# A Hymba layer on one core: units of the feed-forwards in a new input order, FFN1's down groups of 3, 4 and 4, and the final norm's scaling taken from PSUM

## The chip, the core and the metric

The kernel runs on one core of one Trainium2 chip. The metric is the device time of one execution in microseconds; the kernel before takes 996.2 us (median of 3 runs, 993.84 to 996.5). A core has five engines that each work through their own instructions in order: TensorE (PE; its weight loads are listed as PEld), VectorE (DVE), ScalarE (ACT), GpSimd (POOL) and SyncE (SP, which here only issues DMAs). They wait for each other through semaphores. Matrix products go from SBUF into banks of PSUM.

## What is computed

One decoder layer on 528 tokens (16 learned meta tokens ahead of 512 inputs) of width 1024, everything in fp32:

```
def swiglu_ffn(h, w_gu, w_down):
    gate, up = jnp.split(h @ w_gu, 2, axis=-1)
    return (jax.nn.silu(gate) * up) @ w_down          # hidden width 2816

h = concatenate([meta, x])
h = h + 0.5 * swiglu_ffn(rms_norm(h, ffn1_norm), ffn1_w_gu, ffn1_w_down)      # FFN1
h = h + hybrid_mixer(rms_norm(h, mix_norm), w_in, conv_w, b_f, ..., w_out)    # convolution + attention
h = h + 0.5 * swiglu_ffn(rms_norm(h, ffn2_norm), ffn2_w_gu, ffn2_w_down)      # FFN2
return rms_norm(h[:, 16:], final_norm)
```

The change is in FFN1, FFN2 and the final norm. The mixer between them (convolution, attention with forget gates, output projection) is not touched.

## The kernel before

**Products.** Activations lie transposed, features on the 128 partitions, tokens in the free dimension. A product in fp32 is made of three matmuls on rounded parts: every operand is split into a high part `hi` and a rest `lo` (`w_hi`, `w_lo` for weights), and hi·hi, hi·lo and lo·hi are added in PSUM. The split of a weight tile is one cast on ScalarE (`w_hi`) and one subtraction on VectorE (`w_lo`). The weights are loaded in each run by SP's DMAs into `raw` tiles.

**Units.** Most of the two feed-forwards is computed in units by Winograd's form of Strassen's scheme: a block of 2x2 sub-blocks with 7 products instead of 8, of which each works on sums of sub-blocks. The tokens are the halves of one side (264 each in FFN1, 256 in FFN2), two neighbouring column tiles of the weights the other. A unit of gates or of ups contracts four pairs of feature tiles (`nj` = 4, 12 matmuls a product); a down unit contracts `nj` pairs of hidden tiles for two output tiles (`m`), so a group of four units covers the width. FFN1 before has a group of 3 pairs after the hidden tiles 6 to 7, a second of 3, then one of 2 and one of 3 at the end.

The weights of a unit come in four versions (`prep`): `nat` (as loaded), `s1`, `s3` and `s24`. Sums are made partly by DMA, partly by VectorE: SP loads the block (`load`), ScalarE copies one quarter of it (`base`, L474), two DMAs on GpSimd's queue add a second quarter onto `s1` and `s3` (`add`, L478), VectorE makes `s2` (L481) and `s4` (L484), and each version is split (`hi` L492, `lo` L496). Between the products ScalarE copies partial results in PSUM with the sign changed: B = -A (L535) and C = -B (L536); TensorE then adds onto these copies. The other operand, sums ("forms") of hidden tiles, is made in `pair_forms` by GpSimd (L379 to L382) and split by L368 and L369.

The first hidden tiles of each feed-forward (`classical`) are computed by ordinary products (L318) with 4 slots each, since the norm's statistics aren't ready yet; meanwhile VectorE prepares the normed input (`x_pair`, L398).

**What sets the order.** `Slots` is an order written by hand. A product of a unit is a slot, a unit has seven (b is its first; the last product of the unit before stands in slot b+1). `sl.at(t, fn, prio)` puts work of the other engines behind slot t, sorted by prio. As every engine takes its instructions in order, an instruction that waits holds up all that stands behind it on its engine. `prep` counts its steps from b: load at b-15, base b-11, add b-10, s2 b-2, s4 b-1, the split of `s24` at b (cast) and b+1 (rest). Tiles come from pools with few buffers: four for `w_hi` and `w_lo`, three for `raw`, two for `s3`.

**The end of FFN1.** After the last down units `fin` prepares the mixer's input for each finished tile of hT: a cast L275 on ScalarE, then L280 on VectorE, a square L289 on ScalarE and its addition L290 on GpSimd.

**The end of the kernel.** The last two hidden tiles of FFN2 are multiplied in four blocks of 128 tokens (L1210). `finish` then takes the row sums of squares (L1222, ScalarE), the multiplication by the norm's gain out of PSUM (L1224, VectorE), the factor r = 1/rms (L1226, L193, L296 to L298), the scaling by r (L1230 on ScalarE for the left half, L1232 on VectorE for the right half), and the output DMAs (L1233), one on ScalarE's queue and one on SP's.

## Time and profile before

| | |
|---|---|
| median of 3 runs | 996.2 us (993.84, 996.2, 996.5) |
| the profiled execution | 994.59 us, of which its span in the trace is 992.6 |
| busy share of the span | PE 96%, DVE 79%, ACT 59%, POOL 35% |
| granted TensorE clock, mean | 0.989 |

The profiled execution is 1.6 us shorter than the median; 2.0 us of it lie around the span. Times in the trace count from the start of the span. FFN1 lasts until about 386 us, the mixer until about 600, FFN2 until about 966, and the rest is the end. A row of a timeline is one or several like instructions on one engine: start, busy time, engine, line, what is written and read, their number, and in brackets how long the engine stood idle before and what ended that. "PEclk" is the granted clock as a share of full speed. TensorE's matmuls overlap, so its busy share is high even while it isn't at its best; its idle time is what has to be looked at.

### The profile page before, as it was taken

Reading aid. Unit: us, or ns where it says so; the run is one execution under the profiler, and the core shown is the slowest. Engines: PE = TensorE matmul, PEld = TensorE weight load, DVE = VectorE, ACT = ScalarE, POOL = GpSimd, SP = SyncE. Lnnn points to the kernel's source line nnn. Section 1 sums busy time; section 2 is a strip of 40 time slices with the busy share of each in tenths; the row PEclk is TensorE's granted clock in tenths of the full one; section 3 lists DMA queues with packets and bytes.
Section 4 is the critical chain, followed back from the end, with each engine's and each line's share of the span. In section 5 each row is a group of like instructions: output and inputs, shape, how many; then the busy total and the mean of one; then the engine's idle time right before and its main releaser. Section 6 shows DMA issues by size and latency. Waiting matters only on the chain.

```text
span 992.6 us, 17859 instructions
## 1 busy us (share of the span) xinstructions
PE 948.9 (96%) x7022; PEld 905.7 (91%) x7022; DVE 780.0 (79%) x1260; ACT 583.3 (59%) x1036; POOL 345.6 (35%) x319
## 2 busy tenths in 40 slices
PE   9898999999999898999999999999999999999994
PEld 8798999999999887989899978778999999999993
DVE  5688887888788887786777666778887888788764
ACT  5545655665576564775656665446555665667444
POOL 4347533543444563100000000266443553354300
PEclk9999999999999999999999999999999999999998
DMA  6237488668784571532222221247778668787712
GB/s 194 65 107 145 118 174 159 148 120 181 171 151 97 117 142 32 144 103 60 74 66 78 57 84 43 64 137 151 138 157 190 132 133 181 146 180 149 174 29 86
DMA packets 173188, 121.01 MB, mean 122 GB/s; under 512 B 5844, under 2 KB 171520, under 8 KB 173104
## 3 DMA queue, kind: packets, MB, share of 16 engines
q1 hardware_dynamic: 113376, 89.37, 29.6%
q0 software_dynamic: 59008, 28.93, 23.9%
q10 hardware_dynamic: 720, 1.57, 0.4%
q8 instruction: 55, 0.90, 0.4%
q14 instruction: 29, 0.24, 0.1%
HBM read 117.69 MB, written 2.10 MB: 121 GB/s over the span
## 4 chain that ended last, share of the span: by engine, by line
PE 73%; DVE 15%; ACT 5%; issue 4%; DMA 1%; POOL 1%; SPq 0%; ACTq 0%; DVEq 0%
PE bank L522 47%; PE bank L318 20%; DVE w_lo L496 4%; DVE arena L369 2%; PE bank L1055 2%; DMA raw<-in_ffn_w_gu_dram 1%; DVE hT L604 1%; PE bank L1210 1%; DVE w_lo L454 1%; PE bank L992 1%; PE bank L1022 1%; ACT arena L275 1%; DVE w_lo L81 1%; DVE xn L398 1%; PE acc L318 1%
## 5 line engine op out<-in xcount | busy, mean ns | idle before, releaser
L522 PE MATMUL bank<-arena,w_hi 128*128 128x256 f32 (+1 forms) x3080 | 567.7, 286 | 13.3 <-ACT bank L536 7.7
L522 PEld LDWEIGHTS bank<-arena,w_hi 128*128 128x128 f32 x3080 | 481.7, 191 | 19.7 <-ACT bank L536 11.4
L522 PE MATMUL bank<-arena,w_lo 128*128 128x264 f32 (+1 forms) x1540 | 439.1, 285 | 4.2 <-DVE w_lo L496 4.2
L522 PEld LDWEIGHTS bank<-arena,w_lo 128*128 128x128 f32 x1540 | 294.6, 191 | 5.5 <-DVE w_lo L496 5.2
L492 ACT CAST w_hi<-raw 128x1024 fp32r<-128x1024 f32 (+2 forms) x186 | 176.3, 948 | 137.1 <-DVE raw L484 109.7
L318 PE MATMUL bank<-arena,w_hi 128*128 128x264 f32 (+2 forms) x1152 | 246.6, 322 | 2.6 <-ACT w_hi L450 2.6
L496 DVE TENSOR_TENSOR w_lo<-raw,w_hi 128x1024 fp32r<-128x1024 f32 (+2 forms) x186 | 222.9, 1199 | 25.8 <-ACT w_hi L492 24.2
L318 PEld LDWEIGHTS bank<-arena,w_hi 128*128 128x128 f32 x1152 | 178.9, 190 | 18.4 <-ACT w_hi L450 3.0
L318 PE MATMUL bank<-arena,w_lo 128*128 128x264 f32 (+2 forms) x576 | 155.0, 323 | 5.3 <-DVE w_lo L454 5.3
L318 PEld LDWEIGHTS bank<-arena,w_lo 128*128 128x128 f32 x576 | 96.2, 190 | 15.8 <-DVE w_lo L454 8.2
L478 POOL DMA_DIRECT2D raw<-in_ffn_w_gu_dram x34 | 44.1, 1297 | 82.2 <-DMA raw<-in_ffn_w_gu_dram 81.2
L478 POOL DMA_DIRECT2D s<-in_ffn_w_gu_dram x34 | 50.6, 1489 | 61.0 <-ACT bank L536 60.2
L80 ACT CAST w_hi<-raw 128x1024 fp32r<-128x1024 f32 (+3 forms) x54 | 44.1, 828 | 45.9 <-PE bank L318 36.0
L81 DVE TENSOR_TENSOR w_lo<-raw,w_hi 128x1024 fp32r<-128x1024 f32 (+2 forms) x53 | 55.3, 1052 | 18.0 <-ACT w_hi L80 17.7
L478 POOL DMA_DIRECT2D s<-in_ffn_w_down_dram x28 | 41.2, 1472 | 69.1 <-ACT bank L536 63.5
L604 DVE TENSOR_TENSOR hT<-bank,hT 128x264 f32<-128x264 f32 (+1 forms) x112 | 47.5, 424 | 14.9 <-PE bank L522 14.1
L496 DVE TENSOR_TENSOR w_lo<-s,w_hi 128x512 fp32r<-128x512 f32 (+2 forms) x62 | 46.8, 755 | 0.0
L193 ACT ACTIVATE s<-s 128x256 f32<-128x256 f32 (+3 forms) x42 | 19.3, 460 | 46.1 <-DVE s L561 26.7
L474 ACT COPY s<-raw 128x512 f32<-128x512 f32 (+2 forms) x62 | 35.5, 572 | 18.5 <-DVE w_lo L496 15.6
L481 DVE TENSOR_TENSOR raw<-raw 128x512 f32<-128x512 f32 (+2 forms) x62 | 41.4, 669 | 0.8
L369 DVE TENSOR_TENSOR arena<-ts,arena 128x1056 fp32r<-128x1056 f32 (+1 forms) x29 | 35.9, 1237 | 7.5 <-ACT arena L368 7.5
L478 POOL DMA_DIRECT2D raw<-in_ffn_w_down_dram x28 | 35.4, 1264 | 15.2 <-DMA raw<-in_ffn_w_down_dram 14.5
(229 smaller groups left out, 1158.0 us busy)
## 6 DMA issues: line engine op xcount, KB each, us to landing
raw<-in_ffn_w_gu_dram SPq DMA_DIRECT2D x34, 1024.0 KB, 7.0
raw<-in_ffn_w_down_dram SPq DMA_DIRECT2D x20, 768.0 KB, 4.4
raw<-in_w_in_dram SPq DMA_DIRECT2D x24, 512.0 KB, 4.0
raw<-in_ffn_w_gu_dram POOLq DMA_DIRECT2D x34, 256.0 KB, 4.7
s<-in_ffn_w_gu_dram POOLq DMA_DIRECT2D x34, 256.0 KB, 6.3
raw<-in_ffn_w_gu_dram SPq DMA_DIRECT2D x16, 512.0 KB, 4.0
raw<-in_ffn_w_down_dram SPq DMA_DIRECT2D x4, 1024.0 KB, 5.1
raw<-in_ffn_w_down_dram POOLq DMA_DIRECT2D x20, 192.0 KB, 4.4
```

Of the source, the lines that this page charges most:

```text
L80: nc.scalar.copy(h, src)
L81: nc.vector.tensor_sub(lw, src, h.bitcast(F32))
L318: nc.tensor.matmul(ap, lhsT=wt[:, kw, :], rhs=mt[:, k, c0 - off:c1 - off], start=(first and a == 0 and b == 0), stop=(last and a == len(ks ...
L369: self.sl.at(t + 1, lambda: nc.vector.tensor_sub(lo, src(), hi.bitcast(F32)), 2)
L474: nc.scalar.copy(raw["s3"], raw["all"][:, 0::2, 0])
L478: nc.gpsimd.dma_start(out=t, in_=mat_j[:, i, :, c0 + P:c0 + 2 * P], accum_op=ALU.add)
L481: nc.vector.tensor_add(raw["all"][:, 0::2, 0], raw["all"][:, 0::2, 1], raw["all"][:, 0::2, 0])
L492: nc.scalar.copy(w[nm_][0][:, :m], src(nm_))
L496: nc.vector.tensor_sub(w[nm_][1][:, :m], src(nm_), w[nm_][0][:, :m].bitcast(F32))
L522: nc.tensor.matmul(bank, lhsT=wt[:, idx(j), :], rhs=r[:, form, part], start=(start and i == 0), stop=(i == last), skip_group_check=True)
L604: return lambda: nc.vector.tensor_add(t, ps, t)
L1055: nc.tensor.matmul(oo, lhsT=lt, rhs=rt, start=(a == 0 and n_ == 0), stop=(a == 1 and n_ == len(ops) - 1))
```

## The change

1. **Inside a unit** (`prep`): `base` and `add` come two slots later, `s2` and `s4` and the split of `s24` one slot sooner. In the first unit of each feed-forward `nat`, `s2`, `s4` and `s24` come one further slot sooner.
2. **Classical weights** (`prep_classical`): load, cast and rest three slots sooner.
3. **FFN1's opening**: the pool of FFN1 is opened earlier; the weights of hidden tile 2 are loaded in the first stage and split there (`split_raw2`); the gains are transposed and copied sooner.
4. **FFN1's groups**: down groups of 3, 4 and 4 pairs instead of 3, 3, 2 and 3, that is 12 units instead of 16. The gates of tile 14 stand ahead of the second group, its ups behind it. The forms of the last hidden pair are made by `last_pair`, its sums on VectorE, directly ahead of the last group, whose first unit takes its products in the order T2, B21, T1 instead of B21, T2, T1 (`late`).
5. **FFN2's end**: the last two weight tiles are loaded 12 and 11 slots sooner, and split 2 slots sooner.
6. **`finish`**: in the first three blocks r is applied together with the gain, in one VectorE instruction out of PSUM for each half; the output DMAs go to SP, except the left half of the last block.

```diff
-            self.sl.at(t - 8, load, 3)
-            self.sl.at(t - 2, hi, 3)
-            self.sl.at(t - 1, lambda: nc.vector.tensor_sub(w["w"][1], w["r"], w["w"][0].bitcast(F32)), 3)
+            self.sl.at(t - 11, load, 3)
+            self.sl.at(t - 5, hi, 3)
+            self.sl.at(t - 4, lambda: nc.vector.tensor_sub(w["w"][1], w["r"], w["w"][0].bitcast(F32)), 3)
...
             sl.at(b - 15, load, 3)
-            sl.at(b - 11, base, 3)
-            sl.at(b - 10, add, 3)
-            sl.at(b - 2, s2, 3)
-            sl.at(b - 1, s4, 3)
-            for nm_, t in (("nat", b - 4), ("s24", b), ("s1", b + 1), ("s3", b + 2)):
+            sl.at(b - 9, base, 3)
+            sl.at(b - 8, add, 3)
+            c = b - 1 if self.p4 is None else b
+            sl.at(c - 3, s2, 4)
+            sl.at(c - 2, s4, 3)
+            for nm_, t in (("nat", c - 4), ("s24", c - 1), ("s1", b + 1), ("s3", b + 2)):
...
+            for p in (p6, p2, p5) if late else (p2, p6, p5):
+                sl.slot(p)
...
+        def last_pair(self, j, b):
...
+            def split(f, n, s, t):
+                hi, lo = (r[:, f:f + n, i] if n > 1 else r[:, f, i] for i in range(2))
+                sl.at(t, lambda: nc.scalar.copy(hi, s()), 0)
+                sl.at(t + (f in (F_B22, F_T1)), lambda: nc.vector.tensor_sub(lo, s(), hi.bitcast(F32)), 0)
...
+            split(F_B11, 1, lambda: src(0, 0), b + 3)
+            split(F_B22, 1, lambda: src(1, 1), b + 6)
+            sl.at(b + 7, sums, 0)
+            split(F_T1, 3, lambda: v["t"][:, :3], b + 7)
+            sl.at(b + 9, lambda: nc.vector.tensor_sub(v["t"][:, 3], src(1, 0), v["t"][:, 1]), 0)
+            split(F_B21, 1, lambda: src(1, 0), b + 9)
+            split(F_T4, 1, lambda: v["t"][:, 3], b + 9)
...
+            wts2 = [split_raw2(0)]
+            row_rstd(sa)
             table(SILU_SET)
+            out_of(a3)
+            wts2.append(split_raw2(1))
...
         g_units(range(8, 14))
+        F.gates(14)
         for m in range(0, ND, 2):
-            F.down(3, 3, m)
-        g_units(range(14, NF))
+            F.down(3, 4, m)
+        t = F.ups(14)
+        F.hidden_pair(7, t, t)
+        g_units(range(16, NF - 2))
+        F.gates(NF - 2)
+        F.ups(NF - 2)
+        F.last_pair(NF // 2 - 1, len(sl.pe) - 7)
         for m in range(0, ND, 2):
-            F.down(6, 2, m)
-        for m in range(0, ND, 2):
-            for i, t in enumerate(F.down(8, 3, m)):
+            for i, t in enumerate(F.down(7, 4, m, m == 0)):
...
-                sl.at(n - 10 + 6 * i, W.load, 4)
-                sl.at(n - 4 + 3 * i, lambda: W.split(False), 4)
+                sl.at(n - 22 + 7 * i, W.load, 4)
+                sl.at(n - 6 + 3 * i, lambda: W.split(False), 4)
...
-                    nc.vector.tensor_mul(zs[b], pss[i][b], gb[:, b * 512:(b + 1) * 512])
+                    if i == 3:
+                        nc.vector.tensor_mul(zs[b], pss[i][b], gs[b])
...
-                    if b == 0:
+                    if i < 3:
+                        stt(zs[b], pss[i][b], r, gs[b], ALU.mult, ALU.mult)
+                    elif b == 0:
                         nc.scalar.mul(zs[b], zs[b], r)
...
-                    (nc.scalar, nc.sync)[b].dma_start(out=out[i * P:(i + 1) * P, b * 512:(b + 1) * 512], in_=zs[b])
+                    (nc.scalar if i == 3 and b == 0 else nc.sync).dma_start(out=out[i * P:(i + 1) * P, b * 512:(b + 1) * 512], in_=zs[b])
```

**ScalarE in FFN1's first group of three pairs.** In the kernel before, these rows stand on ScalarE in one unit (L474 is the base copy of a later unit, L536 is C = -B, L589 a copy out of PSUM, L535 the next B = -A):

```order
L492 CAST w_hi<-s_1033 128x512
L492 CAST w_hi<-raw 128x768
L474 COPY s_1277<-raw 128x384
L536 ACTIVATE bank<-bank 128x264
L589 COPY ssum<-bank 128x264
L492 CAST w_hi<-raw 128x768
L535 ACTIVATE bank<-bank 128x264
```

The changed kernel has on ScalarE in the same place (L499 is the base copy, L564 C = -B, L617 the copy out of PSUM, L563 B = -A):

```order
L517 CAST w_hi<-s_1068 128x512
L517 CAST w_hi<-raw 128x768
L564 ACTIVATE bank<-bank 128x264
L617 COPY ssum<-bank 128x264
L499 COPY s_1309<-raw 128x384
L517 CAST w_hi<-raw 128x768
L563 ACTIVATE bank<-bank 128x264
```

The base copy moved from the place ahead of C = -B to the second place behind it.

**VectorE in the last units of FFN1.** In the kernel before, VectorE has these rows in a unit of the last group (L604 are additions into hT, L280 is `fin`'s, the first L496 is the rest of `s24`, the second that of `s1`; names with their numbers):

```order
L604 TENSOR_TENSOR hT_67<-bank_517,hT_67 128x264
L280 SCALAR_TENSOR_TENSOR arena_70<-hT_67,gains_75,arena_70 128x528
L496 TENSOR_TENSOR w_lo_4240<-raw_4061,w_hi_4239 128x768
L604 TENSOR_TENSOR hT_67<-bank_515,hT_67 128x264
L496 TENSOR_TENSOR w_lo_4257<-raw_4061,w_hi_4256 128x768
L604 TENSOR_TENSOR hT_67<-bank_514,hT_67 128x264
L280 SCALAR_TENSOR_TENSOR arena_70<-hT_67,gains_75,arena_70 128x528
```

In the changed kernel VectorE has these (L632 additions into hT, L521 the rests of `s24` and `s1`, now of four pairs):

```order
L632 TENSOR_TENSOR hT_67<-bank_532,hT_67 128x264
L521 TENSOR_TENSOR w_lo_4039<-raw_3790,w_hi_4038 128x1024
L280 SCALAR_TENSOR_TENSOR arena_70<-hT_67,gains_75,arena_70 128x528
L632 TENSOR_TENSOR hT_67<-bank_530,hT_67 128x264
L521 TENSOR_TENSOR w_lo_4076<-raw_3790,w_hi_4075 128x1024
L632 TENSOR_TENSOR hT_67<-bank_529,hT_67 128x264
L280 SCALAR_TENSOR_TENSOR arena_70<-hT_67,gains_75,arena_70 128x528
```

The rest of `s24` has moved ahead of L280.

**VectorE in FFN1's opening.** Before, VectorE goes from the norm's factor (L297, L298) to the first classical weights (L454) and the first hidden tiles (L749 to L754) in this order:

```order
L297 SCALAR_TENSOR_TENSOR tt<-sm,tt 128x264
L298 SCALAR_TENSOR_TENSOR rs<-tt,y_482 128x264
L454 TENSOR_TENSOR w_lo<-raw,w_hi 128x1024
L749 SCALAR_TENSOR_TENSOR raw<-raw,rs 128x528
L753 SCALAR_TENSOR_TENSOR raw<-raw,rs 128x528
L754 TENSOR_TENSOR raw<-raw 128x528
L749 SCALAR_TENSOR_TENSOR raw<-raw,rs 128x528
L753 SCALAR_TENSOR_TENSOR raw<-raw,rs 128x528
L754 TENSOR_TENSOR raw<-raw 128x528
L454 TENSOR_TENSOR w_lo<-raw,w_hi 128x1024
L423 SCALAR_TENSOR_TENSOR s<-bank,rs 128x264 x2
```

In the changed kernel VectorE has there (L748 are the two weight tiles split in the first stage, L794 to L799 the first hidden tiles, L479 the next classical weights):

```order
L305 TENSOR_TENSOR arena<-ssum,arena 128x528
L748 TENSOR_TENSOR w_lo<-raw,w_hi 128x1024
L297 SCALAR_TENSOR_TENSOR tt<-sm,tt 128x264
L298 SCALAR_TENSOR_TENSOR rs<-tt,y_501 128x264
L297 SCALAR_TENSOR_TENSOR tt<-sm,tt 128x264
L298 SCALAR_TENSOR_TENSOR rs<-tt,y_501 128x264
L794 SCALAR_TENSOR_TENSOR raw<-raw,rs 128x528
L748 TENSOR_TENSOR w_lo<-raw,w_hi 128x1024
L798 SCALAR_TENSOR_TENSOR raw<-raw,rs 128x528
L799 TENSOR_TENSOR raw<-raw 128x528
L794 SCALAR_TENSOR_TENSOR raw<-raw,rs 128x528
L798 SCALAR_TENSOR_TENSOR raw<-raw,rs 128x528
```

The first rest of a weight tile has moved ahead of the norm's factor, the second one ahead of the first hidden tile's product.

## Rows read from the trace of the kernel before

**Rows 1.** The page: busy time by engine, and one group of instructions with its mean
```profile
PE 948.9 (96%) x7022; PEld 905.7 (91%) x7022; DVE 780.0 (79%) x1260; ACT 583.3 (59%) x1036; POOL 345.6 (35%) x319
...
L496 DVE TENSOR_TENSOR w_lo<-raw,w_hi 128x1024 fp32r<-128x1024 f32 (+2 forms) x186 | 222.9, 1199 | 25.8 <-ACT w_hi L492 24.2
```

**Rows 2.** Stretches: length, then each engine's busy us (count), clock, DMA share, GB/s
```profile
37.20:92.00 54.80, 50.73 (x393) 49.43 (x392) 45.09 (x62) 25.39 (x36) 28.13 (x25) 0.97 0.44 114
92.00:105.00 13.00, 10.53 (x74) 10.31 (x73) 11.20 (x14) 8.35 (x15) 7.71 (x9) 0.87 0.68 119
325.00:386.00 61.00, 52.26 (x399) 49.23 (x397) 52.81 (x98) 35.90 (x67) 31.02 (x30) 1.00 0.54 105
386.00:390.00 4.00, 4.00 (x18) 3.67 (x17) 4.00 (x7) 0.91 (x3) 1.73 (x1) 0.57 0.00 0
610.00:674.90 64.90, 60.63 (x260) 47.85 (x259) 54.79 (x71) 34.92 (x51) 26.89 (x24) 1.00 0.35 95
674.90:687.30 12.40, 10.33 (x73) 10.13 (x72) 11.04 (x13) 6.96 (x12) 8.10 (x7) 0.86 0.70 127
717.60:752.10 34.50, 33.64 (x275) 32.88 (x274) 30.56 (x55) 19.60 (x34) 14.97 (x12) 1.00 0.74 161
913.20:953.60 40.40, 40.40 (x338) 40.38 (x337) 32.23 (x48) 21.05 (x31) 10.65 (x7) 1.00 0.67 138
980.00:992.60 12.60, 0.00 (x0) 0.00 (x0) 4.62 (x12) 5.55 (x16) 0.00 (x0) 0.64 0.33 125
```

**Rows 3.** All waits of an engine by what ended them: us, times, longest
```profile
PE bank L522 <- ACT bank L536: 7.7, 16, 1.2
...
PE bank L522 <- ACT bank L535: 4.9, 3, 2.5
PE bank L522 <- DVE w_lo L496: 4.2, 4, 1.8
```

**Rows 4.** Timeline around 225: start, us, engine, line, operation [idle before <-releaser]; ACT, then PE
```profile
224.72 0.51 ACT L474 COPY s<-raw 128x384 f32<-128x384 f32 x1 [1.00 <-DVE w_lo L496]
...
225.57 0.52 PE L522 MATMUL bank<-arena,w_hi 128*128 128x264 f32 x2 [0.47 <-ACT bank L536]
...
226.04 0.41 PE L522 MATMUL bank<-arena,w_hi 128*128 128x264 f32 x2
```

**Rows 5.** Timeline at the first unit of FFN1: VectorE, then ScalarE
```profile
91.39 2.11 DVE L481 TENSOR_TENSOR raw<-raw 128x512 f32<-128x512 f32 x1
93.53 1.12 DVE L484 TENSOR_TENSOR raw<-raw 128x512 f32<-128x512 f32 x1
...
94.74 1.04 ACT L492 CAST w_hi<-raw 128x1024 fp32r<-128x1024 f32 x1 [4.35 <-DVE raw L484]
```

**Rows 6.** Timeline of FFN1's last down units: VectorE, then GpSimd
```profile
360.99 0.77 DVE L280 SCALAR_TENSOR_TENSOR arena<-hT,gains,arena 128x528 fp32r<-128x528 f32 x1 [1.70 <-ACT arena L275]
361.67 0.95 DVE L496 TENSOR_TENSOR w_lo<-raw,w_hi 128x768 fp32r<-128x768 f32 x1
...
382.90 2.09 DVE L496 TENSOR_TENSOR w_lo<-raw,w_hi 128x768 fp32r<-128x768 f32 x1
...
382.86 1.31 POOL L290 TENSOR_TENSOR ssum<-ssum,sq 128x528 f32<-128x528 f32 x1 [5.79 <-ACT sq L289]
```

**Rows 7.** Timeline of the tail: VectorE, then ScalarE
```profile
980.68 1.41 DVE L1224 TENSOR_TENSOR zg<-bank,ts 128x512 f32<-128x512 f32 x2 [1.37 <-ACT sq L1222]
...
983.43 0.72 ACT L1230 ACTIVATE zg<-zg,t 128x512 f32<-128x512 f32 x1 [0.42 <-DVE t L298]
...
984.62 0.60 ACT L1222 ACTIVATE sq<-bank 128x512 f32<-128x512 f32 x1 [0.47 <-ACT zg L1230]
```

**Rows 8.** An accumulating DMA on GpSimd, VectorE's sum, and the page's landing time
```profile
270.09 1.30 POOL L478 DMA_DIRECT2D raw<-in_ffn_w_gu_dram  x1
...
280.68 0.69 DVE L481 TENSOR_TENSOR raw<-raw 128x512 f32<-128x512 f32 x1
...
raw<-in_ffn_w_gu_dram POOLq DMA_DIRECT2D x34, 256.0 KB, 4.7
```

More of the change, by code (lines that the diff above doesn't have):

```diff
@@ L506, in prep, with products @@
             return w
-        def products(self, nj, rhs, w):
+        def products(self, nj, rhs, w, late=False):
             sl, h = self.sl, self.h
@@ L717, in layer, with split_raw2, out_of @@
+        with tc.manual_schedule(engines={mybir.EngineType.PE, mybir.EngineType.Activation, mybir.EngineType.DVE}):
+            def split_raw2(i):
+                w = (wts.tile([P, 8, P], F32R, name="w_hi"), wts.tile([P, 8, P], F32R, name="w_lo"))
+                nc.scalar.copy(w[0], raw2[i])
+                nc.vector.tensor_sub(w[1], raw2[i], w[0].bitcast(F32))
+                return w
+            def out_of(acc):
                 t = t528("raw")
-                a3.each(lambda ps, g: nc.scalar.copy(g(t), ps))
+                acc.each(lambda ps, g: nc.scalar.copy(g(t), ps))
@@ L719, in layer @@
                 raws_f.append(t)
-            gp = ps1s.tile([P, 512], F32, name="sm")
-            nc.tensor.transpose(gp[:, :36], gt, ident[:36, :36])
-            nc.vector.tensor_copy(gains[:, 8:], gp[:, :36])
-            nc.vector.tensor_scalar(ghalf, gains[:, :24], -0.5, None, ALU.mult)
+            for j in range(3):
+                out_of(accs[j])
+            h, lo = split2(ssum, L)
+            a3, _ = new1()
+            mm(a3, W.take(3), range(4), xh, xl, last=False)
+            sms = [ps1s.tile([P, 512], F32, name="sm") for _ in range(2)]
```

66 lines of the change are left out of this document (37 added, 29 removed).

## The prediction

> **What bounds the kernel now.** I read the page first: TensorE is busy for 948.9 of 992.6 us and VectorE for 780.0 [rows 1]. The change alters no matrix product's size, so the question is where TensorE stands still, and the table by stretches answers it: length minus PE's busy time is what a stretch loses, and PEclk below 1 says that part of the busy time ran at the lower clock. In the product units of the feed-forwards nothing is lost where four pairs are contracted (40.40 busy of 40.40), and almost everything is lost in six kinds of places [rows 2]:
> - the opening of FFN1, 37.2 to 105: 4.07 + 2.47 us idle;
> - a group of four down units with three pairs, 717.6 to 752.1: 0.86 us. There are four such groups (FFN1's first two, FFN2's first two);
> - the last 61 us of FFN1, 325 to 386: 8.74 us, and just behind it 4 us at a clock of 0.57;
> - the opening of FFN2, 610 to 687.3: 4.27 + 2.07 us;
> - the tail, 980 to 992.6, in which PE has nothing left.
>
> The clock costs more on top. At 386 to 390 PE is busy all 4.00 us at 0.57 [rows 2], so (1 - 0.57) x 4.00 = 1.7 us of work is missing there; 13.00 x 0.13 = 1.7 at 92 to 105, 12.40 x 0.14 = 1.7 at 674.9 to 687.3, and 54.80 x 0.03 = 1.6 at 37.2 to 92 come from the same rows. Each of these drops, to the lower of the clock's two levels (1.2 instead of 2.4 GHz), lies behind a long standstill: L535's waits are up to 2.5 us long and `w_lo`'s up to 1.8, while the L536 waits, at most 1.2 [rows 3], leave the clock at 1.00 between 325 and 386. Idle time (6.5 + 4 x 0.86 + 8.7 + 6.3 = 25.0 us) and clock (6.7) make 31.7 us that are to be had ahead of the tail. Restarting costs a little besides: the first pair of matmuls after the gap at 225.57 takes 0.52 us, the next one 0.41 [rows 4]; 0.11 over some thirty gaps is 3 us, which I keep for the bounds.
>
> Then the list of waits, for PE: 7.7 us in 16 waits end with L536, ScalarE's copy C = -B; 4.9 in 3 with L535, the copy B = -A; 4.2 in 4 with VectorE's `w_lo` (L496) [rows 3]. All three are short instructions that come late because of what stands ahead of them on their in-order engines, and that is what the change touches.
>
> **The change part by part.** *The order inside a unit.* At 224.72 ScalarE's base copy L474 waits 1.00 us for VectorE and takes 0.51; L536 stands behind it, and PE starts at 225.57 after a gap of 0.47 [rows 4]. The copy is not urgent, L536 is. Behind L536 the copy holds up nobody that PE reads within a product. So the gaps of these four groups should shrink to nearly nothing, also in the second, which now takes four pairs: 0.86 and three restarts make 1.2 in each, and of that I take 1.05, four times: **4.2** (bounds 0 and 4.8). Moving s24's cast a slot up has a price to check: its buffer is the one that the previous unit's s24 leaves after that unit's last product, so ScalarE may now wait there for PE. Behind it on ScalarE stands the next B = -A, which needs the product after that one anyway, and that product hides the wait; I take 0. With that cover gone a unit loses what an L535 wait costs here, 4.9 / 3 = 1.6 [rows 3].
>
> *The first unit of each feed-forward.* At 91.39 VectorE's two sums take 2.11 and 1.12 us; ScalarE waits 4.35 for them at 94.74 with the cast of s24, and L535 stands behind that cast [rows 5]. This is the 2.47 us gap, and the 1.7 of clock behind it. The sums go one slot up, two for a first unit, a slot being one product, 40.40 / 28 = 1.44 us [rows 2]: the gap goes, and the lower clock with it.
>
> *FFN1's opening as a whole.* The first waits disappear if the weights of f = 2 are loaded and split during the first stage; their two DMAs and the two small operations on the gains that move with them find room there. Later weights are split three slots sooner. All of it would be 6.5 + 3.3 = 9.8, with eight restarts 10.7. But VectorE is busy 45.09 of 54.80 and 11.20 of 13.00 [rows 2], and only one split (1.2 us by the mean of [rows 1]) moves ahead of 37.2. For PE to save 9.8 of 67.8 us VectorE would have to do 55.1 us of work in 58.0: 95%, while it also waits for others. I take **7.5** (bounds 3 and 10.7).
>
> *FFN2's opening.* 6.3 idle and 1.7 of clock, 8.0, but VectorE has 54.79 + 11.04 us of work in 77.3, so there is room on average, and little near the end, 11.04 of 12.40 [rows 2]. Only the three slots are new here, nothing is split ahead of the stage. Loads three slots sooner are the same issues on SP in another place. I take **4.5** (bounds 1.5 and 8).
>
> *FFN1's last group.* Before: eight units, two pairs and then three pairs each, where every fixed cost of a unit (two bank copies, five additions into hT, the wait for the next weights) falls on products of 0.7 to 1.1 us. Afterwards four units of four pairs, the same number of matmuls, and units of this size lose nothing in FFN2 [rows 2]. The second cause there: VectorE stands at L280 for 1.70 us until ScalarE's L275 and the `w_lo` of s24 stands behind it [rows 6]; the new order puts that `w_lo` ahead of L280. The wait then falls on L280, which nobody waits for at once. What remains: the last hidden pair is now made directly ahead of its use, on VectorE, and the first of the four units must wait for the forms; the late order (T2 before B21 and T1) hides a part. I leave 2.4 of 8.74 + 1.7 + a dozen restarts (1.3) = 11.7: **9.3** (bounds 4 and 11.7).
>
> At the same place stands the dearest single row: `w_lo` took 2.09 us beside GpSimd's addition L290, which started 0.04 us earlier and took 1.31; alone it took 0.95 [rows 6]. The Trainium skill ("SBUF — State Buffer", section "SBUF: two separate sides") says that VectorE and GpSimd share a port pair as an exclusive lock, and the one that comes second is blocked for the other's whole instruction; the row agrees, 0.95 + 1.27 = 2.22 against 2.09. The row speaks against the change: the additions L290 stay where they are, and an earlier `w_lo` may meet one as well. By the row each such meeting costs 1.14 us of VectorE; three of them, 3.4, are why I leave 2.4 rather than 1.
>
> *The tail.* The fourth block's squares start at 984.62, behind ScalarE's scaling L1230 (0.72) of the block before [rows 7], though PE has nothing left after 980.0 [rows 2]. Without scaling and DMA issue on ScalarE the squares start at 980.0: 4.6 sooner. SP, which now issues seven of the eight output DMAs, has nothing else to do there. Against it: VectorE's two scaled multiplications of the third block (as long as the two L1224, 1.41 together [rows 7]) may stand in front of the fourth block's own, which I price at 0.9; and the split of the last weights now stands ahead of the last hidden values on VectorE, up to 1.2 [rows 1], taken at 0.7. **3.0** (bounds 1.5 and 4.6).
>
> Sum: 4.2 + 7.5 + 4.5 + 9.3 + 3.0 = 28.5. (The first unit's gap is inside the two openings.) 994.59 - 28.5 = 966.1 for an execution like the profiled one; the median of the three runs stands 1.6 above it, 996.2, so a median between 966 and 968: I say **967**, and give the rivals the same 1 us over their sums.
>
> **Rivals.** *VectorE becomes the bound of both openings.* For it: the 95% above. Then only the first wait and its clock (3.3) and 1.5 in FFN2 are won: 4.2 + 3.3 + 1.5 + 9.3 + 3.0 = 21.3, some **974**. Against: part of its waits there are for ScalarE and TensorE, and shrink when these are earlier.
> *The last group keeps its waits* (chains through ScalarE, the collisions with L290, the late pair): 4 instead of 9.3, **972**.
> *Everything goes*: all idle time, clock and restarts, 4.8 + 10.7 + 8 + 11.7 + 4.6 = 39.8: **955**. Against it stand the full VectorE and the late pair.
> *Slower: the accumulated weights land too late.* GpSimd's add at 270.09 is issued behind four sums and lands 4.7 us later by the median, 274.8; VectorE's sum of it is at 280.68 [rows 8]. A slot less leaves 4.5 of 5.9 us. If the base copies, now two slots later (2.9 us), push the whole GpSimd queue back by that and slow landings add 2.6 more, the sum waits 1 us in each of the 58 units left, and 58 - 28.5 = 29.5: **1025**. It decides from a shift of 4.5 us on, and the add that follows a base copy is not the one that the sum needs.
>
> **How the numbers follow.** The forecast 0.47 with its own range 961 to 972, VectorE in the openings 0.24, the last group 0.14, everything 0.10, late adds 0.03, no effect (waits only move) 0.02. The two middle rivals together reach 979, the third 955, with the unshown pieces (restarts, tail) 2 us on either side: 953 to 981 holds about 0.9 of this by the cases, 0.8 with what I have not thought of. Three runs of this kernel lie 0.27% apart, so 0.3% (3 us) is what counts as a change: faster 0.95, same 0.02, slower 0.03.
>
> **What would show it.** Right: no PE wait for C = -B above 0.3 us in groups of three pairs; no clock below 1.00 at the start of the first unit of either feed-forward; the last four down units of FFN1 at 10.2 us each but for the first, which may take 12; the fourth block's squares in the tail within 0.3 us of its last matmul. Wrong: VectorE over 95% busy with PE still waiting for `w_lo` in the openings (first rival); L280 or L290 in front of late weights (second); VectorE's sums waiting for a DMA (fourth).

## The result and the profile after

The changed kernel takes 973.45 us (median of 4 runs, 971.88 to 973.75) against 995.4 for the kernel before (4 runs); the ratio is 0.9777, with a 95% interval of 0.9759 to 0.9796. That is 22 us faster, inside the range of 953 to 981, but outside the likeliest case's own range of 961 to 972: less than the 28.5 that the sum had come to. The profiled execution took 973.75 us with a span of 972.0, 20.6 less than before.

The page of the changed kernel: span and busy time by engine. Line numbers have moved: the products are L548, B = -A is L563, C = -B L564, `w_lo` L521, additions into hT L632.

```profile
span 972.0 us, 17714 instructions
...
PE 941.5 (97%) x7022; PEld 903.7 (93%) x7022; DVE 773.5 (80%) x1215; ACT 577.3 (59%) x1007; POOL 336.3 (35%) x307
```

TensorE is at 97% instead of 96% [rows 1], VectorE at 80% instead of 79%. Where the 20.6 us lie is seen by cutting both traces at the first matmul of the same stage:

| stage | before, us | after, us | change | forecast |
|---|---|---|---|---|
| start, to the sums for FFN1's norm | 34.5 | 35.9 | +1.4 | 0 |
| FFN1's opening, to the first down group | 81.7 | 76.2 | -5.6 | -7.5 |
| first down group (three pairs) | 33.2 | 33.2 | 0.0 | -1.05 |
| from there to the mixer's sums: second group, last group | 251.9 | 240.7 | -11.3 | -10.35 |
| mixer | 228.4 | 230.2 | +1.9 | 0 |
| FFN2's opening, to its first down group | 87.9 | 87.1 | -0.7 | -4.5 |
| FFN2's two groups of three pairs | 64.9 | 64.2 | -0.8 | -2.1 |
| FFN2's other units | 171.1 | 170.6 | -0.5 | 0 |
| from the last ups to the end | 39.0 | 34.0 | -5.0 | -3.0 |

The stretches of the changed kernel that answer to [rows 2] (length, busy us of PE, PEld, DVE, ACT, POOL, clock, DMA share, GB/s): FFN1's opening in two parts, its three down groups, FFN2's first unit, one of its groups of three pairs, and the tail.

```profile
35.90:86.30 50.40, 50.40 (x415) 50.40 (x414) 45.27 (x60) 25.26 (x37) 27.68 (x23) 1.00 0.44 121
86.30:101.00 14.70, 10.82 (x75) 10.40 (x74) 12.35 (x13) 9.56 (x16) 7.07 (x8) 0.88 0.45 89
112.00:145.20 33.20, 31.62 (x257) 31.20 (x256) 30.62 (x55) 18.24 (x31) 15.54 (x12) 1.00 0.86 178
216.60:257.60 41.00, 41.00 (x339) 41.00 (x338) 31.77 (x48) 22.31 (x33) 10.32 (x8) 1.00 0.77 158
329.60:377.30 47.70, 44.59 (x353) 43.22 (x353) 41.90 (x64) 27.72 (x45) 16.77 (x18) 1.00 0.36 63
656.70:673.00 16.30, 11.45 (x73) 11.04 (x72) 15.85 (x16) 8.72 (x14) 12.59 (x11) 0.79 0.70 126
703.30:735.40 32.10, 31.10 (x258) 30.69 (x257) 28.76 (x52) 17.38 (x30) 14.83 (x12) 1.00 0.75 164
963.80:972.00 8.20, 0.42 (x2) 0.00 (x1) 3.53 (x8) 2.23 (x8) 0.00 (x0) 0.82 0.34 129
```

Three things are to be seen. The first part of FFN1's opening has no idle time left (50.40 of 50.40) and the four units of four pairs have none either (41.00 of 41.00). The first unit of either feed-forward is worse than before: 3.9 us idle at a clock of 0.88 and 4.9 at 0.79, against 2.47 at 0.87 and 2.07 at 0.86 [rows 2]. And the groups of three pairs still stand idle for 1.6 and 1.0 us, more than before: FFN2's first lost 0.86 [rows 2], and FFN1's first 0.94:

```profile
116.20:149.40 33.20, 32.26 (x257) 31.38 (x256) 29.76 (x53) 18.25 (x31) 15.04 (x12) 1.00 0.72 160
```

PE's waits in the changed kernel, which answer to [rows 3]:

```profile
PE bank L548 <- ACT bank L563: 8.3, 6, 3.4
PE bank L548 <- DVE w_lo L521: 4.9, 6, 2.0
PE bank L548 <- DVE hT L632: 2.1, 3, 1.1
```

The waits for C = -B, 7.7 us in 16 before, are gone from the list altogether. In their place stand B = -A with 8.3 us in 6 instead of 4.9 in 3, and the additions into hT, 2.1 us.

What the first unit of FFN1 waits for, on GpSimd, then ScalarE, then TensorE (answers to [rows 5]):

```profile
79.53 2.64 POOL L378 TENSOR_TENSOR ts<-xn 128x264 f32<-128x264 f32 x1
...
85.09 1.21 POOL L381 TENSOR_TENSOR ts<-xn,ts 128x264 f32<-128x264 f32 x1
...
86.34 1.07 ACT L368 CAST arena<-ts 128x1056 fp32r<-128x1056 f32 x1 [3.38 <-POOL ts L381]
89.40 1.04 ACT L517 CAST w_hi<-raw 128x1024 fp32r<-128x1024 f32 x1 [1.98 <-DVE raw L509]
...
90.87 0.37 ACT L563 ACTIVATE bank<-bank 128x264 f32<-128x264 f32 x1
...
91.29 0.51 PE L548 MATMUL bank<-arena,w_hi 128*128 128x264 f32 x2 [3.40 <-ACT bank L563]
```

GpSimd makes the sums of the last normed pair until 86.3. ScalarE stands 3.38 us for them, because the cast of that pair's T forms is ahead in its order; VectorE's rest of those forms and then s4 (L509) follow, ScalarE waits 1.98 for s4, casts s24 and only then makes B = -A. Before, s4 itself was late; now it is what stands ahead of it.

In FFN2 the same wait has another source. ScalarE stands 3.49 us for the sums of a hidden pair (`hd`), not of the last normed pair (`xn`); GpSimd, then ScalarE:

```profile
657.95 1.71 POOL L381 TENSOR_TENSOR ts<-hd,ts 128x256 f32<-128x256 f32 x1
...
659.69 1.05 ACT L368 CAST arena<-ts 128x1024 fp32r<-128x1024 f32 x1 [3.49 <-POOL ts L381]
```

The second unit of the first down group, on VectorE, ScalarE and TensorE:

```profile
118.93 0.99 DVE L506 TENSOR_TENSOR raw<-raw 128x384 f32<-128x384 f32 x1
...
120.53 1.04 DVE L369 TENSOR_TENSOR arena<-s,arena 128x264 fp32r<-128x264 f32 x2
121.49 0.55 DVE L509 TENSOR_TENSOR raw<-raw 128x384 f32<-128x384 f32 x1
121.96 0.76 DVE L632 TENSOR_TENSOR hT<-bank,hT 128x264 f32<-128x264 f32 x2
...
122.12 0.83 ACT L517 CAST w_hi<-raw 128x768 fp32r<-128x768 f32 x1 [3.53 <-DVE raw L509]
...
123.84 0.37 ACT L563 ACTIVATE bank<-bank 128x264 f32<-128x264 f32 x1
...
122.43 0.51 PE L548 MATMUL bank<-arena,w_hi 128*128 128x264 f32 x2 [1.12 <-DVE hT L632]
...
124.26 0.51 PE L548 MATMUL bank<-arena,w_hi 128*128 128x264 f32 x2 [0.46 <-ACT bank L563]
```

VectorE does s2 (L506), two rests of a hidden pair's forms (L369) and s4 ahead of the two additions at 121.96, which TensorE waits for at 122.43; ScalarE waited 3.53 for s4, and B = -A, behind it, costs another 0.46. In the other units of these groups nothing is lost.

### The profile page after: what moved, and what is told of

It reads as the page before. It is cut to its first block, busy times and chain, and to the rows that moved or that the text cites. A ratio compares the mean times of both kernels' runs of the same rounds, so it can differ in the third digit from the quotient of the medians.

```text
span 972.0 us, 17714 instructions
## 1 busy us (share of the span) xinstructions
PE 941.5 (97%) x7022; PEld 903.7 (93%) x7022; DVE 773.5 (80%) x1215; ACT 577.3 (59%) x1007; POOL 336.3 (35%) x307
## 4 chain that ended last, share of the span: by engine, by line
PE 71%; DVE 14%; ACT 7%; issue 4%; POOL 2%; DMA 1%; SPq 0%; ACTq 0%; DVEq 0%; POOLq 0%
PE bank L548 53%; PE bank L318 12%; DVE w_lo L521 2%; PE bank L1103 2%; DVE arena L369 2%; DVE w_lo L81 2%; ACT arena L275 1%; DVE w_lo L479 1%; PE bank L1258 1%; PE bank L1070 1%; DMA raw<-in_w_in_dram 1%; ACT arena L368 1%; DVE xn L397 1%; DVE arena L280 1%; PE bank L1040 1%
## 5 line engine op out<-in xcount | busy, mean ns | idle before, releaser
L548 PE MATMUL bank<-arena,w_hi 128*128 128x256 f32 (+1 forms) x3080 | 564.5, 285 | 10.6 <-ACT bank L563 8.3
L548 PEld LDWEIGHTS bank<-arena,w_hi 128*128 128x128 f32 x3080 | 482.1, 191 | 12.9 <-ACT bank L563 9.6
L548 PE MATMUL bank<-arena,w_lo 128*128 128x264 f32 (+1 forms) x1540 | 439.3, 285 | 4.9 <-DVE w_lo L521 4.9
L548 PEld LDWEIGHTS bank<-arena,w_lo 128*128 128x128 f32 x1540 | 294.8, 191 | 6.7 <-DVE w_lo L521 6.6
L517 ACT CAST w_hi<-raw 128x1024 fp32r<-128x1024 f32 (+1 forms) x174 | 174.1, 1000 | 107.3 <-DVE raw L509 63.6
L521 DVE TENSOR_TENSOR w_lo<-raw,w_hi 128x1024 fp32r<-128x1024 f32 (+1 forms) x174 | 215.0, 1236 | 22.1 <-ACT w_hi L517 21.7
L503 POOL DMA_DIRECT2D s<-in_ffn_w_gu_dram x34 | 45.0, 1325 | 116.5 <-ACT s L499 108.4
L81 DVE TENSOR_TENSOR w_lo<-raw,w_hi 128x1024 fp32r<-128x1024 f32 (+2 forms) x53 | 56.1, 1069 | 15.6 <-ACT w_hi L80 15.3
L503 POOL DMA_DIRECT2D s<-in_ffn_w_down_dram x24 | 32.4, 1352 | 85.1 <-ACT s L499 84.9
L632 DVE TENSOR_TENSOR hT<-bank,hT 128x264 f32<-128x264 f32 (+1 forms) x96 | 39.6, 423 | 24.5 <-PE bank L548 24.0
L563 ACT ACTIVATE bank<-bank 128x256 f32<-128x256 f32 (+1 forms) x58 | 21.5, 370 | 47.0 <-PE bank L548 46.8
L521 DVE TENSOR_TENSOR w_lo<-s,w_hi 128x512 fp32r<-128x512 f32 (+1 forms) x58 | 47.5, 819 | 0.0
L368 ACT CAST arena<-ts 128x1056 fp32r<-128x1056 f32 (+1 forms) x28 | 29.6, 1057 | 29.8 <-POOL ts L381 29.8
L506 DVE TENSOR_TENSOR raw<-raw 128x512 f32<-128x512 f32 (+1 forms) x58 | 39.8, 687 | 3.2 <-DMA raw<-in_ffn_w_down_dram 1.3
L509 DVE TENSOR_TENSOR raw<-raw 128x512 f32<-128x512 f32 (+1 forms) x58 | 39.7, 684 | 0.7
L369 DVE TENSOR_TENSOR arena<-ts,arena 128x1056 fp32r<-128x1056 f32 (+1 forms) x28 | 34.6, 1237 | 5.3 <-ACT arena L368 4.7
```

The lines of the kernel that those rows point to most:

```text
L81: nc.vector.tensor_sub(lw, src, h.bitcast(F32))
L368: self.sl.at(t, lambda: nc.scalar.copy(hi, src()), 2)
L369: self.sl.at(t + 1, lambda: nc.vector.tensor_sub(lo, src(), hi.bitcast(F32)), 2)
L503: nc.gpsimd.dma_start(out=t, in_=mat_j[:, i, :, c0 + P:c0 + 2 * P], accum_op=ALU.add)
L506: nc.vector.tensor_add(raw["all"][:, 0::2, 0], raw["all"][:, 0::2, 1], raw["all"][:, 0::2, 0])
L509: nc.vector.tensor_add(raw["all"][:, 1::2, 0], raw["all"][:, 0::2, 0], raw["all"][:, 1::2, 0])
```

## Experiments

Each was timed in three rounds beside the kernel before; the changes of a stage below come from one profiled execution of each, cut like the table. Most stages agree within 0.1 us where the kernels are alike, but the openings do not: in the five profiles whose openings are built alike (the changed kernel and runs 3, 6, 7 and 8), FFN1's took 74.8 to 76.2 us and FFN2's 87.1 to 87.9. So a difference of 1.4 us in FFN1's opening, or of 0.7 in FFN2's, shows nothing by itself.

**1. The last normed pair's sums on VectorE.**

```diff
-                nc.gpsimd.tensor_sub(t[:, 0], b11, b12)
+                eng.tensor_sub(t[:, 0], b11, b12)
...
-            self.pair_forms(self.xform(j), ..., t + 1, t + 1, 3)
+            self.pair_forms(self.xform(j), ..., t + 1, t + 1, 3, eng=nc.vector if j == 3 else nc.gpsimd)
```

> The changed kernel, with the four sums of the last normed pair (x_pair 3 of each FFN) made by VectorE instead of GpSimd. Theory (chain): in both openings C's and A's copies wait behind ScalarE's cast of that pair's T forms, which waits for GpSimd's sums (3.38 us in FFN1, 3.49 in FFN2). Then the wait of 3.40 us at FFN1's first unit falls below 1.5 and its lower clock goes, likewise 2.81 in FFN2: 965 to 969 us. Rival (VectorE has no time left): four more operations of 0.4 us on VectorE in each opening make both later, 974 to 977 us.

Measured: 969.68 us, 0.9739 (0.9723 to 0.9755). The openings went from 76.2 to 74.8 and from 87.1 to 84.9 us; the waits at the first units' second products from 3.40 to 2.05 and from 2.81 to 2.68, while 2.04 us of waiting for the first unit's `w_lo` in FFN2 went. The time fell by 3.8 us, less than the 4.5 to 8.5 of the theory, and the lower clock stayed, in FFN2 for half as long. FFN1's part is within the spread: run 7, whose opening is unchanged, shows 75.0 us and a wait of 2.29. There GpSimd's L378 and L379 take 1.68 and 0.82 us at the same place, not 2.64 and 1.72, and ScalarE doesn't wait for them. FFN2's part is clear of it, but its 2.68 us stay, because run 1 leaves the hidden pair's sums on GpSimd: ScalarE still waits 3.30 us for them. So a chain through GpSimd was part of it, and not all. Both openings of this kernel, as a whole:

```profile
36.10:110.90 74.80, 72.16 (x570) 71.15 (x569) 67.48 (x88) 41.34 (x65) 38.46 (x32) 0.98 0.44 110
614.80:699.70 84.90, 81.33 (x500) 73.26 (x501) 75.68 (x93) 50.21 (x79) 44.73 (x36) 0.98 0.56 128
```

VectorE has four operations more in each opening and is busy 67.48 and 75.68 us, within 0.6 of the changed kernel's:

```profile
35.90:112.00 76.10, 72.10 (x570) 71.17 (x569) 67.29 (x85) 41.55 (x65) 44.78 (x36) 0.98 0.43 108
616.10:703.30 87.20, 81.88 (x500) 74.23 (x501) 75.15 (x89) 50.35 (x79) 49.08 (x40) 0.96 0.55 125
```

So it does four more operations of 0.43 us at hardly any price: other operations must have become shorter. Run 12 takes that up.

**2. ScalarE no longer held by GpSimd.**

```diff
-            self.pair_forms(self.xform(j), ..., t + 1, t + 1, 3)
+            self.pair_forms(self.xform(j), ..., t + 1, t + 1, 6 if j == 3 else 3)
```

> The changed kernel, with the T forms of the last normed pair cast three slots later on ScalarE and their rests three slots later on VectorE; amounts of work unchanged. Theory (chain, ScalarE held in order by GpSimd): s24's cast and B = -A no longer stand behind the wait, the first unit starts its second product 2 to 4 us sooner in each FFN, unless the T2 product of that unit waits instead: 967 to 971 us. Rival (VectorE has no time left): the same work in another order, 972.5 to 974.5 us.

Measured: 974.26 us, 0.9785 (0.9767 to 0.9803), in the rival's range. FFN1's opening came to 74.4 us, 0.4 below the shortest unchanged one, FFN2's to 90.9, 3.8 longer. There TensorE waits 8.45 us, once, for B = -A: ScalarE stands 9.44 us for GpSimd's sums of the hidden pair, which follow VectorE's postponed rest, and that one stands behind a sum which waits 3.22 us for an accumulating DMA. Another order moves the wait, and can lengthen the stage; it does not take the wait away.

**3. Hidden pairs ahead of the groups of three pairs a unit later.**

```diff
-                    F.hidden_pair(f // 2, t, t, ...)
+                    u = t + (7 if f in (6, 12) else 0)
+                    F.hidden_pair(f // 2, u, u, ...)
```

> The changed kernel, with the forms of the hidden pairs made directly ahead of the three d3 groups one unit (7 slots) later. Theory (VectorE is crowded by those forms in the second unit, so that the additions into hT and s4 come late): the waits in the second units (1.12 + 0.46, 0.53 + 0.47, 0.50 + 0.47 us) go or halve: 970 to 972 us. Rival (s2 and s4 alone, standing ahead of the additions, make the wait): they stay within 0.2 us, 973 to 974 us.

Measured: 971.01 us, 0.9752 (0.9736 to 0.9768). The first group of FFN1:

```profile
112.40:144.40 32.00, 31.53 (x257) 31.12 (x256) 30.47 (x54) 18.15 (x31) 13.97 (x12) 1.00 0.89 185
```

The three groups of three pairs take 32.06, 31.45 and 31.39 us instead of 33.20, 32.09 and 32.09, together 2.5 less, which is the whole difference. The theory holds: those forms crowd VectorE in just that unit.

**4. Only the base copy later, on the kernel before.**

```diff
-            sl.at(b - 11, base, 3)
-            sl.at(b - 10, add, 3)
+            sl.at(b - 9, base, 3)
+            sl.at(b - 8, add, 3)
```

> The kernel before, with only the base copy and the accumulating DMAs two slots later. Theory: this part alone takes away the waits for C = -B in units of two and three pairs, 0.86 us and three restarts in each of four groups and most of 3.9 us in FFN1's last group: 988 to 991 us. Rival (the sums s2 and s4 must come sooner too, or the wait moves to another instruction): 994 to 996 us.

Measured: 989.16 us, 0.9933 (0.9912 to 0.9953). The first groups of three pairs of FFN1 and FFN2:

```profile
117.80:149.80 32.00, 31.64 (x258) 31.22 (x257) 29.26 (x53) 18.32 (x31) 15.00 (x12) 1.00 0.84 181
715.10:746.60 31.50, 31.11 (x257) 30.70 (x256) 28.90 (x53) 18.17 (x31) 14.94 (x12) 1.00 0.76 165
```

They take 32.0 and 31.5 instead of 33.2 and 32.5, 1.2 and 1.0 less, just what the prediction had put for them. So the copy was the cause of the waits for C = -B, and the change as a whole gave much of the gain back: of 1.2 and 1.0 us in these two groups it keeps 0.0 and 0.4.

**5. With less of VectorE's work in the first units.** To runs 1 and 3 together:

```diff
-            F.hidden_pair(j, n0 + 5 * j - 4, n0 + 5 * j - 4, True)
+            F.hidden_pair(j, n0 + 5 * j - 1, n0 + 5 * j - 1, True)
...
-            F.hidden_pair(0, n0 - 5, n0 - 5, True)
-            F.hidden_pair(1, n0 + 1, n0 + 1, True)
+            F.hidden_pair(0, n0 + 8, n0 + 8, True)
+            F.hidden_pair(1, n0 + 13, n0 + 13, True)
```

> The changed kernel with three moves: the last normed pair's sums on VectorE (as in the first experiment), the hidden pairs ahead of d3 groups a unit later (as in the third), and the forms of the hidden pairs 1 and 2 of FFN1 and 0 and 1 of FFN2 later, out of the first unit. The first two alone add up to 967 us. Theory (VectorE has no time left in the openings once GpSimd's chain is gone): with less work for VectorE there, the waits of 2.0 and 2.7 us at the first units' second products fall below 1 and both lower clocks go: 961 to 965 us. Rival (what remains is the path from the sums to s24's cast itself): 966 to 968 us.

Measured: 967.69 us, 0.9702 (0.9679 to 0.9725).

```profile
36.20:110.90 74.70, 70.67 (x570) 69.68 (x569) 67.67 (x90) 42.04 (x66) 38.88 (x33) 1.00 0.50 118
613.70:698.50 84.80, 80.59 (x500) 71.97 (x501) 75.02 (x93) 50.23 (x79) 43.42 (x37) 1.00 0.56 129
```

FFN2's first unit lost its wait (0.46 us; it takes 9.3 us instead of 13.1 in run 1), FFN1's keeps the 2.05 of run 1, and both openings run without the lower clock (1.00). But they are as long as in run 1, 74.7 and 84.8: the units behind wait for what was put off (0.95 and 0.96 us in FFN1, 1.47 and 0.94 in FFN2). The time came out as the rival had it, for a reason that neither had named: that VectorE's work has to be done before the first down group wherever it stands fits this, and run 9 tests it.

**6. The sums at their old slots.** `nat` stays where the changed kernel has it.

```diff
-            c = b - 1 if self.p4 is None else b
+            c = b - 1 if self.p4 is None else b + 1
```

> The changed kernel, with s2, s4 and the split of s24 at the slots of the kernel before in all units but the first of each FFN; the base copy stays two slots later. Theory (the sums a slot sooner are what crowds VectorE in d3 groups, and pay only in FFN1's last group): the d3 groups take 32.0, 31.5 and 31.5 us instead of 33.2, 32.1 and 32.1, and FFN1's last group loses 2 to 6 us because s24's rest stands behind L280 again: 973 to 977 us in all. Rival (the sums sooner help nowhere): 970.5 to 971.5 us.

Measured: 974.0 us, 0.9765 (0.9744 to 0.9786). The first down group and FFN1's last one:

```profile
109.70:141.70 32.00, 31.63 (x258) 31.21 (x257) 29.27 (x53) 18.42 (x31) 14.20 (x12) 1.00 0.85 183
325.80:379.70 53.90, 47.86 (x357) 45.48 (x356) 42.95 (x64) 27.57 (x45) 17.64 (x18) 0.97 0.31 55
```

The groups of three pairs take 31.98, 31.51 and 31.51, as in run 4, 2.4 less in all. The last group, with the part up to the mixer's sums, takes 5.6 more, and part of it runs at the lower clock. Its four units take 14.5, 11.7, 12.8 and 12.7 us instead of 11.8, 11.0, 11.3 and 11.7: 2.7 us of the loss lie in the first unit, where `last_pair` has its work and `fin` none yet, and 3.2 in the three with `fin`. So the sums a slot sooner pay in the last group, only in part for the reason named, and cost where a hidden pair comes between. That the total is level has other reasons besides: in this profile the mixer is back at 228.4, and FFN1's opening and the start are 1.3 and 1.0 us shorter.

**7. The old finish.** The diff is the last part of the change, undone.

> The changed kernel with the finish of the kernel before. Theory (the scaling out of PSUM on VectorE is all of the gain in the tail): the time from the last matmul to the end goes from 8.2 back to 13.0 us, 978 to 979 us. Rival (the earlier split and loads of the last weights carry a part): 975 to 977 us.

Measured: 977.26 us, 0.9797 (0.9778 to 0.9816). From the last matmul to the end:

```profile
962.60:975.40 12.80, 0.40 (x2) 0.00 (x0) 4.61 (x12) 5.60 (x16) 0.00 (x0) 0.70 0.33 123
```

It is 12.8 us instead of 8.2, nearly as the theory had it; the median, 3.8 above the changed kernel's, lies between the two forecasts. From the last ups to the end the kernel takes 4.6 us more: of the tail's gain of 5.0 the finish carries 4.6.

**8. The last hidden pair's forms made as those of the others.**

```diff
-        F.ups(NF - 2)
-        F.last_pair(NF // 2 - 1, len(sl.pe) - 7)
+        t = F.ups(NF - 2)
+        F.hidden_pair(NF // 2 - 1, t, t)
```

> The changed kernel with the last hidden pair's forms made as those of the others (sums on GpSimd, splits later), the late order of the first unit kept. Theory (groups of four pairs need this pair at once, and GpSimd's sums take some 6 us more): the first unit of FFN1's last group waits 3 to 8 us, 977 to 981 us. Rival (its forms are needed last in each product and come in time): 973 to 975 us.

Here the first unit of the last group multiplies by forms that are written behind it, so it waits for nothing, and what it computes isn't the layer. Measured: 973.1 us, 0.9755 (0.9734 to 0.9776). It says nothing of the wait that it was made for; it says that `last_pair` costs nothing against a kernel that does not wait for this pair: the stretch from behind the first down group to the mixer's sums takes 240.7 us with it and 0.3 more without.

**9. More work for VectorE.**

```diff
-            self.sl.at(t + 1, lambda: nc.vector.tensor_sub(lo, src(), hi.bitcast(F32)), 2)
+            for _ in range(2 if twice else 1):
+                self.sl.at(t + 1, lambda: nc.vector.tensor_sub(lo, src(), hi.bitcast(F32)), 2)
```

> The changed kernel, with the rests of the T forms of the second and third normed pair made twice on VectorE (the same result; 2 x 1.24 us more of VectorE's work in each opening, on no other engine). Theory (VectorE's amount of work sets the length of both openings, whatever its order): each opening grows by 2 to 2.7 us, 977.5 to 979 us. Rival (GpSimd's sums and what waits for them set it, VectorE has room): each grows by less than 0.8 us, 973.5 to 975 us.

Measured: 976.84 us, 0.9784 (0.9763 to 0.9805).

```profile
35.20:112.90 77.70, 72.44 (x571) 71.28 (x570) 70.62 (x87) 41.29 (x65) 42.32 (x36) 0.98 0.42 106
617.00:706.00 89.00, 81.88 (x500) 73.58 (x501) 77.40 (x91) 50.24 (x79) 48.92 (x40) 0.96 0.54 123
```

The openings grew from 76.15 to 77.67 and from 87.14 to 89.03 us, by 1.5 and 1.9 for 2.5 of added work: under the theory's bound and over the rival's; against the spread of unchanged openings it is 1.5 to 2.9 and 1.2 to 1.9. VectorE has a little room, about a third of the added work by the profile shown. By the ratios alone the run can't be told from the changed kernel (0.9784 and 0.9777): the reading rests on the openings.

**10. Classical weights at the old slots.**

```diff
-            self.sl.at(t - 11, load, 3)
-            self.sl.at(t - 5, hi, 3)
+            self.sl.at(t - 8, load, 3)
+            self.sl.at(t - 2, hi, 3)
```

> The changed kernel, with load, cast and rest of the classical weights three slots later again, as before. Theory (VectorE's amount of work sets the openings): the classical parts lose what they had won, some 3 us in each FFN, the first units win it back, and the whole stays within 1.5 us: 972 to 975 us. Rival (earlier weights are worth what they save in the classical part): 976 to 980 us.

Measured: 972.63 us, 0.9743 (0.9725 to 0.976). The classical parts took 3.9 and 4.6 us longer than in the changed kernel, the openings as a whole 77.8 (+1.6) and 87.4 (+0.2). What the earlier weights save is given back behind the classical part, nearly all of it in FFN2 and 2.3 of 3.9 us in FFN1. The time is in the theory's range and no longer than the changed kernel's, but not for that alone: the mixer is 1.8 us shorter in this profile and the first down group 0.6.

**11. What pointed to less, together.** Runs 1 and 3, and run 6 for units of three pairs alone:

```diff
-            c = b - 1 if self.p4 is None else b
+            c = b - 1 if self.p4 is None else b + (nj == 3)
```

> The changed kernel with the last normed pair's sums on VectorE, the hidden pairs ahead of d3 groups a unit later, and s2, s4 and s24 at the old slots in units of three pairs only. Theory (the parts add up: 967.2 for the first two, the d3 groups go from 32.1, 31.4 and 31.4 to about 31.1, 30.7 and 30.7 us): 964.5 to 966 us. Rival (the later pair and the later sums take away the same wait): 967 to 968 us.

Measured: 965.62 us, 0.9673 (0.9656 to 0.969). The groups of three pairs take 31.30, 30.89 and 30.88 us and have no wait over 0.2 us left, as the theory had it; the two causes add.

**12. All sums of the normed pairs on VectorE.** One word of run 11 is changed: `eng=nc.vector`.

> The combined kernel of the run before, with the sums of all four normed pairs of each FFN on VectorE. Theory (GpSimd's sums lengthen the operations of VectorE that run beside them by about what they take off it): VectorE's busy time in the openings grows by less than 2 us in each instead of 3 x 1.7 = 5.1, and the time stays within 2 us of 965.6: 964 to 967.5 us. Rival (GpSimd's sums are a true relief): 3 us and more later in each opening, 971 to 975 us.

Measured: 964.19 us, 0.9679 (0.9659 to 0.9698), in the theory's range and not to be told from run 11 by the intervals; both beat the changed kernel. The openings:

```profile
35.20:110.10 74.90, 71.45 (x571) 71.02 (x570) 67.83 (x103) 41.56 (x65) 23.10 (x20) 0.98 0.47 115
612.40:695.90 83.50, 80.87 (x499) 73.28 (x500) 74.66 (x105) 49.25 (x78) 29.61 (x25) 0.98 0.58 131
```

They take 74.9 and 83.5 us, with twelve operations of 0.43 us more in each than run 11 has:

```profile
34.70:109.50 74.80, 72.12 (x570) 71.18 (x569) 67.91 (x89) 41.44 (x65) 38.47 (x32) 0.98 0.45 110
611.70:697.30 85.60, 80.23 (x500) 71.90 (x501) 74.90 (x93) 49.09 (x78) 46.34 (x37) 1.00 0.56 127
```

VectorE is busy 67.83 and 74.66 us, against 67.91 and 74.90 in run 11: the 5.2 us of added operations cost it nothing, so others became shorter. One group that shrank, between 36 and 112 us, in the changed kernel and then in this one (count, busy us, mean ns):

```profile
L479 DVE TENSOR_TENSOR w_lo<-raw,w_hi 128x1024 fp32r<-128x1024 f32 x6 | 8.7, 1455 | 0.0
```

```profile
L479 DVE TENSOR_TENSOR w_lo<-raw,w_hi 128x1024 fp32r<-128x1024 f32 x6 | 7.5, 1247 | 0.0
```

A weight's rest takes 1.25 us instead of 1.46 when GpSimd makes no sums of normed pairs beside it. GpSimd's help with these sums costs VectorE about as much as it spares it.

## Why the prediction was right, and where its sum failed

**The base copy ahead of C = -B** (4.2 us in four groups). The mechanism was right: the waits for L536's successor (L564) are gone, and run 4 gives 1.2 and 1.0 a group. The step that failed is that the groups' gaps "should shrink to nearly nothing": the sums that the same change put a slot sooner bunch on VectorE with a hidden pair's forms in the second unit (runs 3 and 6), and three of the four groups of three pairs gained 0.0, 0.4 and 0.4. The second group has four pairs now and loses nothing (41.00 busy of 41.00); before, it took some 1.8 us more than its 255 matmuls would at that pace, and that stands within the 11.3.

**The first units and the openings** (7.5 and 4.5, measured 5.6 and 0.7). "The gap goes, and the lower clock with it" is the step that was wrong. The gap became longer, 3.40 and 2.81 us, and the clock fell as before, because GpSimd's sums and then VectorE itself were late. Earlier weights, and in FFN1 the split ahead of it, bring TensorE sooner to the first unit (7.1 us in FFN1, 4.6 in FFN2), and it waits there. I had VectorE's 95% as a rival with 0.24 and 974 us. The time is almost that rival's, and runs 9, 10 and 5 speak for its mechanism: added work on VectorE lengthens the openings by most of its amount, weights brought sooner are mostly given back, and work put off moves the wait. But it isn't the whole. VectorE was busy for 88% and 86% of the openings, not the 95% set as its sign (only FFN2's first unit reached it, 15.85 of 16.30 us). Run 1 shortens FFN2's opening by 2.3 us though VectorE is as busy, and run 2, an order alone, lengthens it by 3.8: chains between GpSimd, ScalarE and VectorE count too, and how the loss divides stays open. FFN1's opening kept 5.6 because one weight tile is split ahead of it and the waits at 40 and 73 us (2.7 and 1.2) have gone, with the lower clock behind the first; no run undid the split alone.

**FFN1's last group** (9.3, with the second group 10.35; measured 11.3). Both reasons held in part: four-pair units lose nothing in the second group, and the sums and s24 a slot sooner are worth 5.6 us by run 6, of which 3.2 lie in the units where L280 stands. The first unit was forecast at up to 12 us and took 11.8; the other three were forecast at 10.2 and took 11.0, 11.3 and 11.7, since TensorE still waits there for `w_lo` and B = -A (3.1 us idle in the 47.70 us above, where 2.4 had been left). The price of the collisions was about right:

```profile
355.09 0.77 DVE L280 SCALAR_TENSOR_TENSOR arena<-hT,gains,arena 128x528 fp32r<-128x528 f32 x1
...
358.41 1.85 DVE L280 SCALAR_TENSOR_TENSOR arena<-hT,gains,arena 128x528 fp32r<-128x528 f32 x1
...
358.37 1.32 POOL L290 TENSOR_TENSOR ssum<-ssum,sq 128x528 f32<-128x528 f32 x1 [1.30 <-ACT sq L289]
```

L280 takes 1.85 us beside GpSimd's L290 and 0.77 without it, 1.08 more, where [rows 6] gave 1.14 for `w_lo`. The Trainium skill ("SBUF — State Buffer", section "SBUF: two separate sides") has VectorE operations with two SBUF inputs and GpSimd's operations that read SBUF exclude each other for a whole instruction; the row nearly agrees (0.77 and the 1.28 that L290 still had to run make 2.05, and 1.85 was measured), and run 12 fits it.

**The tail** (3.0, measured 5.0). The mechanism was right, and two terms were mis-sized: the fourth block's squares start at 963.24, 1.0 us before the end of the last matmul and not at it, and the split ahead of the last hidden values (0.7) costs nothing, since the part from the last ups to the last matmul is 0.2 us shorter. ScalarE, then VectorE in the changed kernel's tail (answers to [rows 7]):

```profile
963.24 0.58 ACT L1271 ACTIVATE sq<-bank 128x512 f32<-128x512 f32 x1
...
963.84 1.41 DVE L1279 SCALAR_TENSOR_TENSOR zg<-bank,t,ts 128x512 f32<-128x512 f32 x2
965.16 1.28 DVE L1273 TENSOR_TENSOR zg<-bank,ts 128x512 f32<-128x512 f32 x2
```

VectorE's multiplications of the third block do stand in front of those of the fourth, 1.3 us, and on the chain that ended last. Their price of 0.9 was about right: from the fourth block's squares to the end of the span it takes 8.8 us, against 8.0 before.

**What the sum left out.** The start was 1.4 us longer in the profiled execution and the mixer 1.9. The first can't be laid to the change: the changed kernel's start took 34.6 to 36.2 us in the runs above, the old one 34.5 and 35.0. The mixer took 230.1 to 230.4 in nine runs and the changed kernel, and 228.3 to 228.4 in the kernel before and runs 4, 6 and 10. In the changed kernel TensorE waits 0.9 us there for a ScalarE cast (L953). Every profile with the longer mixer has a wait of 0.8 to 1.1 us at that place, and none with the shorter one; what brings it about stays open, and it was not tried by itself.

**The other rivals.** The accumulated weights did not come late: of VectorE's two sums one waited for a DMA, once, for 1.3 us in the whole trace:

```profile
DVE raw L506 <- DMA raw<-in_ffn_w_down_dram: 1.3, 1, 1.3
```

The last group kept 3.1 us of its 8.74 of idle time, far from that rival's sum. "Everything goes" failed in the openings, as had been held against it.

So the forecast lay within its range because errors of both signs met: 8.1 us too much for openings and groups of three pairs, 3.3 us not foreseen in start and mixer, 3.4 too little for the last group, other units and the tail. That it came so close to the first rival's 974 is in part luck as well: that rival had nothing of start and mixer in it.
